# One decoder layer on one core: the embedding's projection moved from the middle to the front and kept in DRAM, the first up slab split earlier, and the gate tiles in another order

## The chip, the core and the metric

The kernel runs on one core of a Trainium2 chip. TensorE (PE) multiplies, VectorE (DVE), ScalarE (ACT) and GpSimd (POOL) work elementwise, and SyncE (SP) issues most transfers. Each has a queue of its own and takes its instructions in order. The metric is the device time of one launch in microseconds; three runs of the kernel before gave 852.27, 852.78 and 852.79, median 852.78.

## The reference

One layer over 512 tokens of 1024 features, all float32 (cut to what matters):

```python
h = _layer_norm(x, ln_in_g, ln_in_b)
proj = h @ w_in[i]
pool_in, qkv, z, beta_raw, a_raw, gate_a, gate_b = jnp.split(proj, SPLIT_POINTS, axis=-1)
y_a = _multiscale_pool(pool_in, pool_w[i], pool_scale[i])
y_b = _gated_deltanet(qkv, z, beta_raw, a_raw, ...)
mixed = jax.nn.sigmoid(gate_a) * y_a + jax.nn.sigmoid(gate_b) * y_b
h = _layer_norm(DEEPNORM_ALPHA * h + mixed @ w_out[i], ln1_g[i], ln1_b[i])
mlp = jnp.square(jax.nn.relu(h @ w_up[i])) @ w_down[i]
r = DEEPNORM_ALPHA * h + mlp
ple = jax.nn.sigmoid(r @ ple_gate_w[i]) * (p[i] @ ple_proj_w[i])
h = _layer_norm(r + ple, ln2_g[i], ln2_b[i])
```

The embedding's projection is `p[i] @ ple_proj_w[i]`: 512x256 by 256x1024. It depends on inputs alone and is used only in the last but one line, so it can be computed anywhere ahead of that. Gate is used below for `sigmoid(r @ ple_gate_w[i])`.

## The kernel before, in words

Every float32 matrix product is computed from split operands: `hi` is the operand rounded to TensorE's fast type (fp32r), `lo` the rest, and three matmuls, hi by hi, hi by lo and lo by hi, replace one. A weight slab therefore costs a transfer into a `raw` tile (512 KB), a cast on ACT to `hi` and a subtraction on DVE to `lo`, each 128 partitions by 1024. Activations that are multiplied stand with features on partitions in `act`, in hi and lo; the tokens of 128 each (four blocks, t = 0 to 3) are brought there by TensorE transposes, an ACT cast and a DVE subtraction (`to_features`, `features`).

In the order of the program:

1. The front: `warm_up` runs fourteen small matmuls on the identity, X comes in eight transfers of 256 KB, `stats` takes each block's mean and variance on DVE, POOL makes `rstd_in` and `nmr` from them, ACT normalises X, PE transposes it (`ps_in`), ACT applies gain and offset (`hf_in`), and `act` gets its hi and lo parts. During the transposes, eight more warm-up matmuls are issued. Then come the first matmuls, `ps_ba` and `ps_k`.
2. The two mixers over all heads, to about 405 us.
3. The output projection (`tok_gemm` with `wo`): weights in eight slabs, four token blocks by two column halves in PSUM; `out_done` adds the residual, does LN1's statistics and leaves the block's result in `res[t]`, followed by `to_features`. Ahead of it p is transposed (`pT`), and behind it the embedding's projection runs: 48 matmuls into `ps_pp`, eight ACT copies into `pproj` in SBUF.
4. The feed-forward network in a loop over eight column groups c of w_up (`up_tile`, `even_block`, `odd_block`) with w_down's pieces x, y, z and w (`fetch`, `onto`, `split_dn`, `product`, `gather`): sums of quarters of w_down are multiplied instead of all quarters, and `gather` puts the products together on DVE. The very first up tiles are computed in two token halves (`HALVES`) in the old form.
5. The end: `features(0)` and `features(1)` transpose the first two token blocks of the result, `product(4)` follows, then the gate's tiles: `gate_tile(t, half)` is 24 matmuls for one token block and one half of the columns. `embed` applies the sigmoid, multiplies with `pproj` and adds; `finish` is LN2.

The code states one order, but instructions are put into each engine's queue by a scheduler that simulates the program. `tc.issue_after(x)` forbids that something is issued ahead of x. PSUM and SBUF tiles come from pools with tags and a number of buffers; the next tile of a tag waits for whoever still reads the buffer that it takes.

## Time and profile before

| | |
|---|---|
| median of three runs | 852.78 us |
| profiled execution, its own time | 852.83 us |
| span of the profiled execution | 851.0 us |
| PE busy | 833.2 us (98%) |
| DVE busy | 605.9 us (71%) |
| ACT busy | 404.0 us (47%) |
| POOL busy | 90.0 us (11%) |
| mean DMA rate | 116 GB/s |

A row of the timeline gives start, length, engine, line of the kernel, operation, and tiles as output<-inputs; in brackets, how long the engine had been idle before and who ended that. Rows of repeated matmuls are folded (x5). The length of one matmul contains its fill, so successive matmuls start closer together than they are long. PEld is the weight load ahead of a matmul, PEclk the clock that TensorE was granted as a part of full speed. The lines themselves stand in the prediction.

### The profile page before, as it was taken

The page shows a single profiled execution, that of the slowest core. Times are in us where ns is not written, and L with a number is a line of the kernel's source. Part 1 is how long each engine was busy: PE and PEld are TensorE (multiplying, and loading weights), DVE is VectorE, ACT ScalarE, POOL GpSimd, SP SyncE. Part 2 cuts the span into 40 slices and gives each one's busy share as a digit, 9 for nine tenths or more (in the row PEclk, how much of TensorE's full clock was granted, in tenths as well). Part 3 has the DMA queues.
Part 4 walks back from the last instruction along what each step waited for, and adds up shares of the span by engine and source line. Part 5 has one row for each costly group of instructions (what it writes and reads, how often), then busy time and mean ns, then how long its engine had stood idle before and what let it go on. Part 6 is the DMA issues. An engine that isn't in the chain of part 4 may idle for free.

```text
span 851.0 us, 12480 instructions
## 1 busy us (share of the span) xinstructions
PE 833.2 (98%) x4848; PEld 693.9 (82%) x4848; DVE 605.9 (71%) x1185; ACT 404.0 (47%) x628; POOL 90.0 (11%) x94
## 2 busy tenths in 40 slices
PE   7999999999999999999999999999999999999996
PEld 5787888888888888888888878888888888888785
DVE  8798968759866635569369394857576767667986
ACT  5566455465563634442207555353545453634510
POOL 4061000001000000110011111111111111010000
PEclk9999999999999999999999999999999999999999
DMA  6313222321321312265316647575757566654221
GB/s 204 99 53 96 83 69 54 97 75 50 84 73 33 109 47 75 81 211 159 125 50 217 155 128 174 140 172 139 179 138 190 133 166 163 156 127 123 75 75 49
DMA packets 73196, 98.45 MB, mean 116 GB/s; under 512 B 4537, under 2 KB 48946, under 8 KB 73138
## 3 DMA queue, kind: packets, MB, share of 16 engines
q1 hardware_dynamic: 64384, 80.87, 30.0%
q0 software_dynamic: 8704, 16.78, 11.9%
q8 instruction: 38, 0.62, 0.3%
q14 instruction: 20, 0.16, 0.1%
q10 hardware_dynamic: 50, 0.01, 0.0%
HBM read 95.56 MB, written 2.10 MB: 115 GB/s over the span
## 4 chain that ended last, share of the span: by engine, by line
PE 90%; DVE 5%; ACT 2%; DMA 1%; issue 1%; POOL 0%; SPq 0%; DVEq 0%; ACTq 0%; POOLq 0%
PE ps_up L844 19%; PE ps_dnx L844 5%; PE ps_pg L844 5%; PE ps_dn L844 5%; PE ps_dny L844 5%; PE ps_dnz L844 3%; PE ps_z L67 2%; PE ps_gb L66 2%; PE ps_z L66 2%; PE ps_ga L67 2%; PE ps_gb L68 2%; PE ps_gb L67 2%; PE ps_z L68 2%; PE ps_ga L66 2%; PE ps_ga L68 2%; PE ps_q L66 1%
## 5 line engine op out<-in xcount | busy, mean ns | idle before, releaser
L844 PE MATMUL ps_up<-act,hi_up 128*128 128x512 f32 x480 | 147.8, 389 | 0.0
L844 PEld LDWEIGHTS ps_up<-act,hi_up 128*128 128x128 f32 x480 | 90.0, 188 | 18.6
L844 PE MATMUL ps_up<-act,lo_up 128*128 128x512 f32 x240 | 93.4, 389 | 0.0
L844 ACT ACTIVATE r<-ps_up 128x512 f32<-128x512 f32 x32 | 19.0, 595 | 102.4 <-PE ps_up L844 99.5
L844 POOL DMA_DIRECT2D x<-in_w_down_dram x24 | 29.0, 1210 | 273.8 <-DVE lo_dn L844 273.8
L844 PEld LDWEIGHTS ps_up<-act,lo_up 128*128 128x128 f32 x240 | 45.0, 188 | 9.4
L844 DVE TENSOR_TENSOR lo_dn<-x,hi_dn 128x1024 fp32r<-128x1024 f32 x32 | 39.0, 1220 | 8.3 <-ACT hi_dn L844 8.3
L844 PE MATMUL ps_dnx<-hi_dn,hid_s 128*128 128x512 f32 x128 | 42.3, 391 | 0.0
L844 ACT CAST hi_dn<-x 128x1024 fp32r<-128x1024 f32 x32 | 33.5, 1048 | 12.2 <-PE ps_dn L844 9.0
L844 ACT CAST hid_s<-r 128x512 fp32r<-128x512 f32 x32 | 18.3, 618 | 41.5 <-DVE r L844 41.5
L844 DVE TENSOR_TENSOR hid_a<-r,hid_a 128x256 fp32r<-128x256 f32 x16 | 6.8, 426 | 41.4 <-ACT hid_a L844 41.4
L844 PE MATMUL ps_pg<-hi_pg,act 128*128 128x512 f32 (+1 forms) x128 | 35.9, 363 | 0.0
L844 DVE TENSOR_TENSOR hid_b<-r,hid_b 128x512 fp32r<-128x512 f32 x16 | 11.1, 692 | 34.0 <-ACT hid_b L844 34.0
L844 DVE TENSOR_TENSOR lo_up<-raw_up,hi_up 128x1024 fp32r<-128x1024 f32 x28 | 33.5, 1217 | 0.0
L844 DVE TENSOR_TENSOR r<-r 128x256 f32<-128x256 f32 x64 | 27.2, 425 | 2.2
L844 ACT CAST hi_up<-raw_up 128x1024 fp32r<-128x1024 f32 x28 | 28.6, 1046 | 0.0
L844 PEld LDWEIGHTS ps_dnx<-hi_dn,hid_s 128*128 128x128 f32 x128 | 23.9, 188 | 5.7 <-DVE hid_s L844 0.4
L844 DVE TENSOR_TENSOR hid_s<-r,hid_s 128x512 fp32r<-128x512 f32 x32 | 20.7, 689 | 11.0 <-ACT hid_s L844 11.0
L844 PEld LDWEIGHTS ps_pg<-hi_pg,act 128*128 128x128 f32 x128 | 23.1, 189 | 3.8
L844 PE MATMUL ps_dnx<-lo_dn,hid_s 128*128 128x512 f32 x64 | 24.9, 389 | 0.0
L577 POOL TENSOR_TENSOR rs<-rs,mhalf 128x4 f32<-128x4 f32 x8 | 9.0, 1131 | 150.0 <-DVE rs L576 150.0
L844 DVE TENSOR_TENSOR res<-ps_dnx,res 128x512 f32<-128x512 f32 x32 | 21.0, 685 | 4.7 <-PE ps_dnx L844 4.7
(734 smaller groups left out, 2397.2 us busy)
## 6 DMA issues: line engine op xcount, KB each, us to landing
raw_up<-in_w_up_dram SPq DMA_DIRECT2D x32, 512.0 KB, 7.9
x<-in_w_down_dram POOLq DMA_DIRECT2D x24, 512.0 KB, 6.1
raw_wo<-in_w_out_dram SPq DMA_DIRECT2D x8, 512.0 KB, 3.5
x<-in_w_down_dram SPq DMA_DIRECT2D x8, 512.0 KB, 9.3
z<-in_w_down_dram SPq DMA_DIRECT2D x8, 512.0 KB
y<-in_w_down_dram SPq DMA_DIRECT2D x8, 512.0 KB, 7.7
w<-in_w_down_dram SPq DMA_DIRECT2D x8, 512.0 KB, 3.5
y<-in_w_down_dram POOLq DMA_DIRECT2D x8, 512.0 KB, 8.8
```

The lines of the kernel that those rows point to most:

```text
L66: T.matmul(ps, wh, ah, start=first, stop=False)
L67: T.matmul(ps, wh, al, start=False, stop=False)
L68: T.matmul(ps, wl, ah, start=False, stop=last)
L577: G.tensor_tensor(out=rs, in0=rs, in1=mhalf.to_broadcast([P, NT]), op=ALU.pow)
L844: return lambda *a, **k: tc.keep_in_program_order(op(*a, **k))
```

## The change

The projection of the embedding moves to the front. Directly behind the warm-up, p and its weights are loaded ahead of X, transposed and split, and `project` computes both halves; each result is copied to SBUF and written to a DRAM tile (`pproj`, eight of 256 KB). In the loop's groups 2 and 3 they are read back into SBUF tiles (`ppb`). The statistics of X, in DVE's queue, are issued behind the projection's subtractions; of those, the second slab's is on POOL. The eight warm-up matmuls among X's transposes go.

In the middle, `first_up` loads the two slabs of the first up tiles in place of the projection's weights and splits them in four pieces during the output projection. X of w_down is split (`split_dn(x, "01")`) ahead of the last two token blocks' features. Both first up tiles compute their first token half ahead of these features, and their second half behind. The tiles of the PSUM pool `pp2` are declared in another order.

At the end `gather(yb, 1, 1, SUB)` is issued ahead of the split of the gate's second slab, and the gate tile of block 1 ahead of `features(2)` and `features(3)`.

```diff
     warm_up(ps_warm, 14)
+    dp = root.enter_context(tc.tile_pool(name="dp", bufs=8, space=bass.MemoryType.DRAM))
+    ptok = mxp.tile([P, NT, 256], F32, tag="big", name="ptok")
+    dma(out=ptok, in_=p[0, 0].rearrange("(t p) c -> p t c", p=P))
+    wraw = []
+    for half in range(2):
+        raw = wp.tile([P, 2, 512], F32, tag="raw", bufs=3, name=f"raw_pp{half}")
...
+    for kb in range(2):
+        ps = tps(f"ps_pT{kb}")
+        for t in range(NT):
+            T.transpose(ps[:, t, :], ptok[:, t, kb * P:(kb + 1) * P], ident)
+        ps = ps.rearrange("p t c -> p (t c)")
+        act_last = A.copy(pT[kb][0], ps)
+        vec_last = V.tensor_tensor(out=pT[kb][1], in0=ps, in1=pT[kb][0].bitcast(F32), op=SUB)
+    wpp = []
+    for half in range(2):
...
+        with tc.issue_after(act_last.ins), tc.issue_after(vec_last.ins):
+            act_last = A.copy(hi, wraw[half])
+            sub = (G if half else V).tensor_tensor(out=lo, in0=wraw[half], in1=hi.bitcast(F32), op=SUB)
+            vec_last = vec_last if half else sub
+        wpp.append((hi, lo))
+    st_last = vec_last
...
+    def project(half):
+        hi, lo = wpp[half]
+        for t in range(NT):
+            ps = gps(f"ps_pp{half}{t}")
+            for kb in range(2):
+                ah, al = pT[kb][0][:, t * P:(t + 1) * P], pT[kb][1][:, t * P:(t + 1) * P]
+                T.matmul(ps, ah, hi[:, kb, :], start=kb == 0, stop=False)
+                T.matmul(ps, ah, lo[:, kb, :], start=False, stop=False)
+                T.matmul(ps, al, hi[:, kb, :], start=False, stop=kb == 1)
+            got = ep.tile([P, 512], F32, tag="E", bufs=8, name=f"ppc{half}{t}")
+            A.copy(got, ps)
+            pproj[t, half] = dp.tile([P, 512], F32, tag="pp", bufs=8, name=f"pproj{half}{t}")
+            dma(out=pproj[t, half], in_=got)
...
     for t in range(NT):
-        with tc.issue_after(st_last.ins) if t else nullcontext():
+        with tc.issue_after(st_last.ins):
             st_last = stats(xts[t], f"in{t}", tp1, mv_in[:, t, :])
...
-            if kb == 3:
-                with tc.issue_after(pe_last.ins):
-                    warm_up(ps_warm, (2, 2, 0, 0)[t])
...
-    pp2.tile([P, SEQ], F32, tag="g", bufs=6, name="ps_g")
...
+    pp2.tile([P, 4, P], F32, tag="tp", bufs=2, name="ps_t")
+    for i in range(2):
+        pp2.tile([P, SEQ], F32, tag="g", bufs=6, name=f"ps_g{i}")
...
+    def first_up(k0):
+
+        raw = wp.tile([P, 4, 256], F32, tag="raw", bufs=3, name=f"raw_up0_0{k0}")
+        dma(out=raw, in_=w_up[0, k0:k0 + 512, 0:256].rearrange("(a p) c -> p a c", p=P))
+        for q in range(2):
+            hi, lo = (ep.tile([P, 2, 256], F32R, tag="E", bufs=8, name=f"{n}_up0_0{k0}{q}") for n in ("hi", "lo"))
+            A.copy(hi, raw[:, 2 * q:2 * q + 2, :])
+            V.tensor_tensor(out=lo, in0=raw[:, 2 * q:2 * q + 2, :], in1=hi.bitcast(F32), op=SUB)
+            ups.append((hi, lo))
...
+        for k0 in (0, 512):
+            first_up(k0)
...
-            to_features(res[t], t, pp2, ("tp",), 2, "l1")
+            if t < 2:
+                to_features(res[t], t, pp2, ("tp",), 2, "l1")
...
+    start = [g3(f"ps_up00{i}") for i in range(2)]
+    for i in range(2):
+        up_tile(start[i], i, ups, HALVES[0])
+    w = {1: split_dn(x, "01")}
+    for t in range(2, NT):
+        features(t, "l1")
...
+        if c in (2, 3):
+            for t in range(NT):
+                got = ep.tile([P, 512], F32, tag="E", bufs=8, name=f"ppb{c - 2}{t}")
+                oS.dma_start(out=got, in_=pproj[t, c - 2])
+                pproj[t, c - 2] = got
...
-    gates = [[ups[0], split_up(raws[1], "pg01")], []]
     product(7, left, w[7], yb, True, True)
     gather(yb, 1, 1, SUB)
+    gates = [[ups[0], split_up(raws[1], "pg01")], []]
...
     first = list(gate_tile(0, 0, whole))
     gather(yb, 1, 0)
+    second = list(gate_tile(1, 0, whole))
     features(2)
     features(3)
-    second = list(gate_tile(1, 0, whole))
```

How instructions stand on the engines, at the three places. First ACT's queue at the front, before: the four blocks of X are normalised (`x`), then the first features (`hf_in`).

```order
L213 ACT_TABLE_LOAD
L213 ACTIVATE x_106<-x_106,nmr,rstd_in 128x1024
L213 ACTIVATE x_109<-x_109,nmr,rstd_in 128x1024
L213 ACTIVATE x_112<-x_112,nmr,rstd_in 128x1024
L213 ACTIVATE x_115<-x_115,nmr,rstd_in 128x512
L219 COPY pcol<-ps_prow 128x25
L233 ACTIVATE hf_in_203<-ps_in_198,pcol 128x512
L195 CAST hi_k_225<-raw_k_144 128x1024
L233 ACTIVATE hf_in_212<-ps_in_207,pcol 128x512
```

In the change, from pT's second cast on (`ppc` are copies of the projection):

```order
L162 CAST hi_pp_132<-raw_pp_110 128x1024
L162 CAST hi_pp_136<-raw_pp_112 128x1024
L179 COPY ppc_193<-ps_pp_186 128x512
L260 ACTIVATE x_140<-x_140,nmr,rstd_in 128x1024
L260 ACTIVATE x_143<-x_143,nmr,rstd_in 128x1024
L179 COPY ppc_204<-ps_pp_197 128x512
L260 ACTIVATE x_146<-x_146,nmr,rstd_in 128x1024
L179 COPY ppc_215<-ps_pp_208 128x512
L260 ACTIVATE x_149<-x_149,nmr,rstd_in 128x512
L266 COPY pcol<-ps_prow 128x25
L179 COPY ppc_226<-ps_pp_219 128x512
L239 CAST hi_k_347<-raw_k_178 128x1024
```

Five of the projection's copies (a fifth follows the last row) and the second cast of k's weights now stand ahead of the first features. On SP, at the program's start, the difference of the two queues:

```order
-L183 DMA raw_ba<-in_w_in_dram 128x8x16
-L183 DMA raw_k_142<-in_w_in_dram 128x4x256
-L183 DMA raw_k_144<-in_w_in_dram 128x4x256
...
+L143 DMA ptok<-in_p_dram 128x4x256
+L147 DMA raw_pp_110<-in_ple_proj_w_dram 128x2x512
+L147 DMA raw_pp_112<-in_ple_proj_w_dram 128x2x512
+L187 DMA x_140<-in_x_dram 128x512 x2
...
+L233 DMA dtb<-in_dt_bias_dram 128x8
+L227 DMA raw_k_176<-in_w_in_dram 128x4x256
+L227 DMA raw_k_178<-in_w_in_dram 128x4x256
+L181 DMA pproj_195<-ppc_193 128x512
```

Three transfers stand ahead of X, and k's weights behind the small loads. Third, PE at the end, before: the end of the first gate tile, the transposes of the last two blocks (`ps_rt`), and the second tile's start.

```order
L844 MATMUL ps_pg_7261<-lo_pg_7246,act 128x512
L844 MATMUL ps_pg_7261<-hi_pg_7245,act 128x512
L844 MATMUL ps_rt_7288<-ident,res_4223 128x128 x4
L844 MATMUL ps_rt_7295<-ident,res_4223 128x128 x4
L844 MATMUL ps_rt_7302<-ident,res_4224 128x128 x4
L844 MATMUL ps_rt_7309<-ident,res_4224 128x128 x4
L844 MATMUL ps_pg_7316<-hi_up_7068,act 128x512
L844 MATMUL ps_pg_7316<-lo_up_7069,act 128x512
```

In the change (`ps_pg_7331` is the second gate tile, `ps_pg_7412` the third, the first with the other half's weights):

```order
L880 MATMUL ps_pg_7331<-lo_pg_7289,act 128x512
L880 MATMUL ps_pg_7331<-hi_pg_7288,act 128x512
L880 MATMUL ps_rt_7356<-ident,res_4326 128x128 x4
L880 MATMUL ps_rt_7363<-ident,res_4326 128x128 x4
L880 MATMUL ps_rt_7370<-ident,res_4327 128x128 x4
L880 MATMUL ps_rt_7377<-ident,res_4327 128x128 x4
L880 MATMUL ps_pg_7412<-hi_pg_7384,act 128x512
L880 MATMUL ps_pg_7412<-lo_pg_7385,act 128x512
```

The transposes have moved behind the second tile, directly ahead of the third. On DVE the order there is as before:

```order
L880 TENSOR_TENSOR act<-ps_rt_7356,act 128x4x128
L880 TENSOR_TENSOR act<-ps_rt_7363,act 128x4x128
L880 TENSOR_TENSOR act<-ps_rt_7370,act 128x4x128
L880 TENSOR_TENSOR act<-ps_rt_7377,act 128x4x128
L880 TENSOR_TENSOR lo_pg_7385<-raw_pg_7296,hi_pg_7384 128x1024
L880 TENSOR_TENSOR lo_pg_7389<-raw_pg_7298,hi_pg_7388 128x1024
```

The third tile's first `lo_pg` (7385) stands behind the four subtractions from `ps_rt`.

More of the change, by code (lines that the diff above doesn't have):

```diff
@@ L7 @@
-from contextlib import ExitStack, nullcontext
+from contextlib import ExitStack
 import concourse.bass as bass
@@ L197, in k0_part @@
         return hi, lo
+    for half in range(2):
+        project(half)
     rstd_in = cst.tile([P, NT], F32, name="rstd_in")
@@ L811, in layer @@
     tok_gemm(w_out[0], lambda kb, i, t: mixed[kb][:, i, t * P:(t + 1) * P], _P2(), "g", "wo", out_done)
-    pproj = {}
-    for half in range(2):
-        hi, lo = load(ple_proj_w[0, :, 512 * half:512 * half + 512].rearrange("(a p) c -> p a c", p=P), 512,
-                      f"pp{half}")
-        for t in range(NT):
-            ps = pp2.tile([P, 512], F32, tag="g", bufs=pp2g, name=f"ps_pp{half}{t}")
-            for kb in range(2):
-                ah, al = pT[:, kb, 0, t * P:(t + 1) * P], pT[:, kb, 1, t * P:(t + 1) * P]
-                T.matmul(ps, ah, hi[:, kb, :], start=kb == 0, stop=False)
-                T.matmul(ps, ah, lo[:, kb, :], start=False, stop=False)
-                T.matmul(ps, al, hi[:, kb, :], start=False, stop=kb == 1)
-            pproj[t, half] = ep.tile([P, 512], F32, tag="E", bufs=8, name=f"pproj{half}{t}")
-            A.copy(pproj[t, half], ps)
     ph2.close()
@@ L849, in g3 @@
         return pp3.tile([P, SEQ], F32, tag="g", bufs=4, name=name)
-    perm = {i: [pp3.tile([P, SEQ], F32, tag="u", bufs=4, name=f"ps_dn{i}_{m}") for m in range(2)]
-            for i in (1, 6)}
     def wide(name):
@@ L899, in split_up, with up_tile @@
         return split(raw, name, wp, ("whi", "wlo"))
-    def up_tile(c, j, i, gr):
-        ps = g3(f"ps_up{c}{j}{i}")
-        ms = slice(i * P, (i + 1) * P)
-        first = c == 0 and j == 0
-        for c0, c1 in (HALVES if first else ((0, SEQ),)):
-            for kb in range(KB):
-                hi, lo = gr[kb // 4]
-                for q, (w, h) in enumerate(((hi, 0), (hi, 1), (lo, 0))):
-                    (T if first else oT).matmul(ps[:, c0:c1], w[:, kb % 4, ms], act[:, kb, h, c0:c1],
-                                                start=kb == 0 and q == 0, stop=kb == KB - 1 and q == 2)
+    def up_tile(ps, i, gr, cut=(0, SEQ)):
+        ms, (c0, c1) = slice(i * P, (i + 1) * P), cut
+        blocks = [(hi[:, j, ms], lo[:, j, ms]) for hi, lo in gr for j in range(hi.shape[1])]
+        for kb, (hi, lo) in enumerate(blocks):
+            for q, (w, h) in enumerate(((hi, 0), (hi, 1), (lo, 0))):
+                oT.matmul(ps[:, c0:c1], w, act[:, kb, h, c0:c1],
+                          start=kb == 0 and q == 0, stop=kb == KB - 1 and q == 2)
         return ps
@@ L962, in gather, with features @@
                 oV.tensor_tensor(out=dst, in0=dst, in1=banks[m], op=SUB)
-    def features(t):
+    def features(t, name="rt"):
         for half in range(2):
-            ps = pp3.tile([P, 4, P], F32, tag="u", bufs=4, name=f"ps_rt{t}{half}")
+            ps = pp3.tile([P, 4, P], F32, tag="u", bufs=4, name=f"ps_{name}{t}{half}")
             for a in range(4):
@@ L988, in layer @@
         left = [None, None]
-        ps = up_tile(c, 0, 0, ups[0:2])
         if fst:
-            w[1] = split_dn(x, f"{c}1")
-            onto(x, c, 0, 1)
+            ps = up_tile(start[0], 0, ups[0:4], HALVES[1])
+            ups += [split_up(raw, f"up0{n}") for n, raw in enumerate(raws)]
         else:
+            ps = up_tile(g3(f"ps_up{c}00"), 0, ups[0:2])
             gather(yb, 1, 0)
@@ L1000, in layer @@
         r2, ha = even_block(c, 0, ps)
-        ps = up_tile(c, 0, 1, ups[0:2])
+        ps = up_tile(start[1], 1, ups[0:4], HALVES[1]) if fst else up_tile(g3(f"ps_up{c}01"), 1, ups[0:2])
         w[2] = split_dn(z, f"{c}2")
@@ L1014, in layer @@
         left[0] = odd_block(c, 0, ps, r2, ha)
-        ps = up_tile(c, 1, 0, ups[2:4])
+        ps = up_tile(g3(f"ps_up{c}10"), 0, ups[-2:])
         if fst:
@@ L1018, in layer @@
         r2, ha = even_block(c, 1, ps)
-        ps = up_tile(c, 1, 1, ups[2:4])
+        ps = up_tile(g3(f"ps_up{c}11"), 1, ups[-2:])
         if fst:
```

25 lines of the change are left out of this document (13 added, 12 removed).

## The prediction

> **What bounds the kernel now.** I read the page's head first, then busy time by stretches, then the chain of waits at the start, then the timeline at the three places that the change touches.
>
> ```profile
> span 851.0 us, 12480 instructions
> ...
> PE 833.2 (98%) x4848; PEld 693.9 (82%) x4848; DVE 605.9 (71%) x1185; ACT 404.0 (47%) x628; POOL 90.0 (11%) x94
> ```
>
> TensorE is busy for 833.2 of 851.0 us. Work that leaves the middle gains its full length, and work that arrives at the front costs its full length, unless it falls into idle time. Where that lies, by stretches (length; busy time of PE, PEld, DVE, ACT, POOL; granted clock, DMA share, GB/s):
>
> ```profile
> 0.00:10.00 10.00, 6.16 (x37) 5.74 (x37) 8.51 (x20) 3.53 (x3) 6.54 (x21) 1.00 0.82 250
> 10.00:15.00 5.00, 2.97 (x21) 2.20 (x21) 3.83 (x8) 3.74 (x6) 2.42 (x5) 0.99 0.62 170
> 15.00:18.00 3.00, 3.00 (x11) 2.18 (x11) 2.28 (x5) 3.00 (x6) 0.00 (x0) 0.50 0.95 318
> ...
> 443.00:467.00 24.00, 23.68 (x149) 20.86 (x148) 22.17 (x32) 14.64 (x23) 4.42 (x3) 1.00 0.54 179
> 467.00:788.00 321.00, 321.00 (x1454) 266.31 (x1453) 212.37 (x291) 158.32 (x219) 38.95 (x32) 1.00 0.62 152
> ```
>
> PE idles 3.84 + 2.03 = 5.87 us in the first 15, and not at all in the 321 us of the feed-forward loop. So the front holds the idle time worth filling. From its chain of waits (start, length, what):
>
> ```profile
> 4.78 4.95 DMA x<-in_x_dram
> ...
> 13.62 0.79 ACT hf_in L233
> ...
> 18.76 0.44 PE ps_in L228 x4
> ```
>
> X's last piece lands at 4.78 + 4.95 = 9.73, and then a serial chain (statistics on DVE, rstd and nmr on POOL, normalising on ACT, transposes on PE) reaches the first features at 13.62.
>
> **The change, part by part. 1. The front.** Durations from the timeline (start, length, engine):
>
> ```profile
> 1.49 4.89 PE L95 MATMUL ps_warm<-ident 128*128 128x128 f32 x28 [1.49 <-POOL ident L81]
> 4.34 1.27 DVE L102 BATCH_NORM_STATS2 st_in<-x 128x6 f32<-128x512 f32 x2
> 5.95 0.24 POOL L208 TENSOR_SCALAR rstd_in<-mv_in 128x1 f32<-128x1 f32 x1 [1.68 <-DVE mv_in L103]
> ...
> 6.94 0.26 POOL L210 TENSOR_SCALAR nmr<-mv_in,rstd_in 128x1 f32<-128x1 f32 x1
> 7.24 1.24 ACT L213 ACTIVATE x<-x,nmr,rstd_in 128x1024 f32<-128x1024 f32 x1 [0.29 <-POOL nmr L210]
> ...
> 12.32 0.82 ACT L213 ACTIVATE x<-x,nmr,rstd_in 128x512 f32<-128x512 f32 x1 [0.70 <-POOL nmr L210]
> ...
> 14.29 1.03 ACT L195 CAST hi_k<-raw_k 128x1024 fp32r<-128x1024 f32 x1
> ...
> 24.41 0.39 PE L66 MATMUL ps_k<-act,hi_k 128*128 128x512 f32 x1
> 24.64 0.39 PE L67 MATMUL ps_k<-act,hi_k 128*128 128x512 f32 x1
> ...
> 26.93 0.39 PE L68 MATMUL ps_k<-act,lo_k 128*128 128x512 f32 x1
> ```
>
> A 512-wide matmul costs 24.64 - 24.41 = 0.227 us where they follow one another. The first k tile ends at 26.93 + 0.39 = 27.3; the front's cost is measured there, because PE is nearly never idle behind it.
>
> SyncE now issues ptok and two raw_pp, 3 x 512 KB, ahead of X. What the DMA engines move when they are full:
>
> ```profile
> 6.00:8.00 2.00, 0.55 (x5) 0.32 (x3) 1.95 (x4) 1.71 (x2) 1.24 (x4) 1.00 0.98 338
> ```
>
> 1.57 MB / 338 GB/s = 4.7 us, at a share of 0.98, so X cannot come beside it: its last piece lands near 14.4. Three engines then carry new work ahead of X. The warm-up ends at 6.4, the eight pT transposes near 7.4; ACT casts pT twice and hi_pp twice (about 0.55 and 1.03 each) to 10.6. DVE subtracts pT twice and splits lo_pp0 to about 10.7, and only then starts the statistics (row 4.34). POOL does lo_pp1 ahead of its first rstd. No row has a 128x1024 subtraction on POOL; the nearest, of 128x512, on POOL and on DVE (busy us, mean ns):
>
> ```profile
> L314 POOL TENSOR_TENSOR gs<-upper,glo 128x512 fp32r<-128x512 f32 x8 | 11.9, 1508 | 28.2 <-DVE glo L298 28.2
> L314 DVE TENSOR_TENSOR gs<-upper,ghi 128x512 fp32r<-128x512 f32 x8 | 6.4, 811 | 0.0
> ```
>
> POOL takes 1.508 / 0.811 = 1.86 times DVE's time. DVE does a 128x1024 in 1.21 (row 810.43 below), so 2.25 us; the ends are 1.2 (as on DVE) and 3.0 (twice 1.508). I take 2.25, by the ratio of one and the same operation.
>
> POOL is through at 10.6 + 2.25 = 12.85; rstd and nmr take 6.94 + 0.26 - 5.95 = 1.25, so X's first normalising starts near 14.1. ACT then runs in order three X blocks (1.24), the last half block (0.82), four copies of the projection (0.55, row 456.38 below), and the second hi_k (1.03), which stood behind the first features before: 3.7 + 0.8 + 2.2 + 1.0 = 7.7. First features near 21.8 instead of 13.62: **+8.2**, a little less as starts lie closer than lengths. By PE instead: when X's second block is ready, near 16.6, PE has ahead of it 30 of the 48 projection matmuls (6.8), 28 transposes (0.44 for four, 3.1) and the 40 matmuls of ba and the first k tile (9.1): 16.6 + 19.0 = 35.6 against 27.3: **+8.3**. I take **+8.0**. In other words: PE gets 48 x 0.227 = 10.9 and eight transposes, 1.0, loses eight warm-up matmuls (8 x 4.89 / 28 = 1.4), and of the 5.87 idle us only 2.5 are filled, since the projection itself must wait for lo_pp0. Ends: +4.7, if all behind X's landing keeps pace, and +10.5, if no idle time is filled.
>
> In SyncE's queue, raw_k now follows the smaller loads and waits for two of the three raw buffers, until lo_pp0 and lo_pp1 are done, near 12.9; with X landing until 14.4 it comes at 17 to 18, ahead of its casts near 19. And raw_v0a stands behind the last write of the projection, which waits for the last copy near 29: 1 us later than the front's shift alone, but its weights are first used at
>
> ```profile
> 46.11 0.40 PE L66 MATMUL ps_v<-act,hi_v0a 128*128 128x512 f32 x1
> ```
>
> so that is nothing. Eight writes of the result and eight reads of it in the feed-forward loop, 256 KB each, add 4.2 MB. The cover is the DMA share of 0.62 in 467-788, with fetches issued some ten us ahead; I cost them at nothing. Without that cover a read costs 0.26 MB / 338 GB/s = 0.8 us.
>
> **2. The middle.**
>
> ```profile
> 404.79 1.04 PE L741 MATMUL ps_pT<-ident,ptok 128*128 128x128 f32 x8
> 406.35 0.53 PE L758 MATMUL ps_wo<-hi_wo,mx 128*128 128x512 f32 x1 [0.52 <-ACT sga L711]
> ...
> 406.98 0.74 DVE L715 SCALAR_TENSOR_TENSOR sga<-ps_lift,pcol,sga 128x512 f32<-128x512 f32 x1
> ...
> 452.13 1.31 PE L822 MATMUL ps_pp<-hi_pp,pT 128*128 128x512 f32 x5
> 452.14 1.07 ACT L118 CAST act<-ps_l 128x512 fp32r<-128x512 f32 x2
> ...
> 455.68 1.28 DVE L119 TENSOR_TENSOR act<-ps_l,act 128x512 fp32r<-128x512 f32 x2
> ...
> 456.38 1.09 ACT L826 COPY pproj<-ps_pp 128x512 f32<-128x512 f32 x2
> ...
> 465.44 0.48 PE L911 MATMUL ps_up<-act,hi_up 128*128 128x256 f32 x2
> ...
> 477.04 0.63 PE L844 MATMUL ps_up<-act,hi_up 128*128 128x512 f32 x2
> ```
>
> The pT transposes (1.04) go, but gain nothing: with the PSUM tiles declared in another order, the first ps_wo lies in the bank that ps_lift held, and waits for DVE's sga, 406.98 + 0.74 = 407.7, instead of 406.35: **+1.4**. All of PE's work is queued behind it. If ACT's sga still ended the wait, it would be 0; those are the ends.
>
> From the last output-projection matmul to the first 512-wide up matmul now pass 477.04 - 452.13 = 24.9 us. In the change: 96 half-width matmuls, 477.04 - 465.44 = 11.6; the 16 transposes of the last two token blocks, 1.7 (804.09 - 802.42 below has sixteen); about 0.75 of waiting for the second block's subtraction, which 10.9 us of projection covered; and about 1.5 behind the last transposes, where a cast (half of 1.07), a subtraction (half of 1.28) and their hand-overs stand bare. Sum 15.5, **-9.4**. The last block's statistics must come earlier for that. They do, as six 128x1024 subtractions leave DVE, which was busy for 22.17 of 24 us; the first half's 5.8 us of up matmuls cover the rest. Ends: no waits, -11.6; and the late X of rival D. Middle together: **-8.0**.
>
> **3. The end.**
>
> ```profile
> 794.15 0.47 PE L844 MATMUL ps_dny<-hi_dn,hid_b 128*128 128x512 f32 x1 [1.30 <-DVE res L844]
> ...
> 802.42 1.91 PE L844 MATMUL ps_rt<-ident,res 128*128 128x128 f32 x16
> 804.09 0.47 PE L844 MATMUL ps_pg<-hi_up,act 128*128 128x512 f32 x1
> ...
> 806.09 2.36 DVE L844 TENSOR_TENSOR lo_pg<-raw_pg,hi_pg 128x1024 fp32r<-128x1024 f32 x2
> ...
> 810.43 1.21 DVE L844 TENSOR_TENSOR lo_pg<-raw_pg,hi_pg 128x1024 fp32r<-128x1024 f32 x1
> ```
>
> The gather goes ahead of one such lo_pg on DVE, so product 4 starts 1.1 earlier, near 793.0. But the second gate tile goes ahead of the transposes of the last two token blocks. A gate tile is 24 x 0.227 = 5.44: the two now end near 801.3 and 806.7, and the transposes start at 806.7 instead of 802.42, 4.3 later. ACT's and DVE's orders are unchanged: the casts and subtractions from ps_rt stand ahead of the splits of the second half's gate weights, which so come 4.3 later too: the first lo_pg is done at 806.09 + 1.2 + 4.3 = 811.6, the third at 810.43 + 1.2 + 4.3 = 815.9; the fourth slab's transfer starts when the first is split, 3.5 us before its own split, which ends near 817.5. The third gate tile ran from 804.09 + 5.44 = 809.5 to 815.0. It could now start at 808.4, waits 3.1 us, stops again for the third and fourth slab, and has five matmuls (1.1) behind 817.5: it ends near 818.6. **+3.6**. What follows keeps that distance. Ends: -1.1 and +4.7, the second if the gather gains nothing.
>
> **Sum:** 8.0 - 8.0 + 3.6 = +3.6 on the profiled execution's 852.83 (span 851.0), which is 0.05 above the median 852.78: **856.4**.
>
> **The rivals.** A: the front costs X's delay alone, +4.7. For it speaks that ACT is busy for only 3.53 + 3.74 of the first 15 us, against it that the projection's copies and the second hi_k are queued in ACT ahead of the features. 4.7 - 8.0 + 3.6: 853.1, no change. B, on the other side: the third gate tile does not stall, and the end keeps its -1.1. Its place is DVE's queue behind the transposes; it decides by whether the first lo_pg is done when PE comes, at 808.4. For it speaks only that ACT and DVE have idle time there; the unchanged queues speak against it. 8.0 - 8.0 - 1.1: 851.7, not slower. A and B together: 848.4. C, the clock: gaps near 3 us arise at ps_wo (407.7 - 404.8) and at the third gate tile. The granted clock was 0.50 in 15-18, behind the front's gaps, which cost 1.5 us of full speed. Twice that: 859.4. [...] D: X of w_down comes late. ACT now splits it ahead of the last features (transfers, KB each, median us to landing):
>
> ```profile
> x<-in_w_down_dram SPq DMA_DIRECT2D x8, 512.0 KB, 9.3
> ...
> w<-in_w_down_dram SPq DMA_DIRECT2D x8, 512.0 KB, 3.5
> ```
>
> At 3.5 us it is there in time, at 9.3 the casts of the last two blocks start 3.9 late: 860.3.
>
> **How the numbers follow.** This kernel's measurement cannot tell a change of about 0.2%, 1.7 us, from none. Chances: forecast 0.47, A 0.12, B 0.13, A with B 0.10, C 0.10, D 0.08. Slower: forecast, C and D, less 0.03 of the forecast's own spread, 0.62. Same: A and some two thirds of B, 0.20. Faster: the rest, 0.18. The range, 849.5 to 860.5, leaves out most of A with B and half of C and D; the forecast's own is 853.5 to 859.
>
> **What would show it.** Right: the first hf_in near 21.5 and the first k tile's end near 35; ps_wo behind DVE's sga; the first 512-wide up matmul at the old time within 1 us; ps_pg with about 3 us of idle time released by lo_pg, near 808. Wrong: X's last piece landing before 12; no wait ahead of the third gate tile; a granted clock below 0.9 in the middle; ACT waiting for X of w_down near 455.

## The result, and the profile after

Four runs of the changed kernel gave 858.39, 860.18, 860.59 and 861.65, median **860.38 us**; the kernel before took 852.78 beside it. The ratio is 1.008, interval 1.0066 to 1.0095: slower by 7.6 us, where 3.6 were forecast. The profiled execution took 860.59, near the median. The page's head:

```profile
span 858.8 us, 12504 instructions
...
PE 833.7 (97%) x4840; PEld 693.3 (81%) x4840; DVE 604.9 (70%) x1186; ACT 403.6 (47%) x630; POOL 92.5 (11%) x95
```

TensorE's busy time is what it was (833.2), though a half-speed stretch at the front (clock 0.50 in 15 to 18 us) has gone and another has come in the middle (0.50 in 419 to 421); nearly all of the 7.8 us of span is new idle time (25.1 against 17.8). The table of waits, TensorE's rows, says where (total, times, longest):

```profile
PE ps_wo L805 <- DVE sga L759: 2.8, 1, 2.8
PE ps_pg L880 <- DVE lo_pg L880: 2.0, 2, 1.3
PE ps_pg L880 <- ACT hi_pg L880: 1.8, 1, 1.8
PE ps_in L275 <- ACT x L260: 1.6, 2, 1.0
PE ps_pp L175 <- ACT hi_pp L162: 1.5, 1, 1.5
...
PE ps_gb L66 <- DVE zs L730: 1.4, 1, 1.4
```

The timeline of TensorE at the places of the forecast (start, length, line, operation, tiles, and in brackets the idle time before and who ended it):

```profile
36.56 0.43 PE L298 MATMUL ps_bat<-ident,bat 32*128 32x32 f32 x4 [0.20 <-ACT bat L295]
...
398.82 0.50 PE L66 MATMUL ps_gb<-act,hi_gb3a 128*128 128x512 f32 x1 [1.43 <-DVE zs L730]
...
418.26 0.69 PE L805 MATMUL ps_wo<-hi_wo,mx 128*128 128x512 f32 x1 [2.83 <-DVE sga L759]
...
421.73 0.44 PE L807 MATMUL ps_wo<-hi_wo,mx 128*128 128x512 f32 x1
...
465.45 0.28 PE L823 MATMUL ps_wo<-hi_wo,mx 128*128 128x256 f32 x1
...
481.09 0.63 PE L880 MATMUL ps_up<-act,hi_up 128*128 128x512 f32 x2
...
796.67 0.47 PE L880 MATMUL ps_dny<-hi_dn,hid_b 128*128 128x512 f32 x1 [0.18 <-DVE res L880]
...
814.08 0.50 PE L880 MATMUL ps_pg<-hi_pg,act 128*128 128x512 f32 x1 [1.77 <-ACT hi_pg L880]
815.34 0.50 PE L880 MATMUL ps_pg<-lo_pg,act 128*128 128x512 f32 x1 [0.76 <-DVE lo_pg L880]
819.66 0.50 PE L880 MATMUL ps_pg<-lo_pg,act 128*128 128x512 f32 x1 [1.28 <-DVE lo_pg L880]
```

The same instructions of the kernel before, and how much later each is now:

| TensorE's instruction | before | after | later by |
|---|---|---|---|
| `ps_bat`, right behind the first k tile | 27.52 | 36.56 | 9.0 |
| first `ps_gb` of slab 3a | 388.34 | 398.82 | 10.5 |
| first `ps_wo` | 406.35 | 418.26 | 11.9 |
| the ninth `ps_wo` | 408.35 | 421.73 | 13.4 |
| last `ps_wo` | 452.01 | 465.45 | 13.4 |
| first up matmul of 512 columns | 477.04 | 481.09 | 4.05 |
| product 4 | 794.15 | 796.67 | 2.5 |
| the third gate tile's last wait | 812.59 | 819.66 | 7.1 |
| end of the span | 851.0 | 858.8 | 7.8 |

So the front cost 9.0, the middle gave back 13.4 - 4.05 = 9.4, and the end cost 7.8 - 4.05 = 3.7: these three the forecast had. Two things it didn't have stand between: 1.5 us at `ps_gb`, and 1.5 us over the first nine `ps_wo`. (From the first wide up matmul to product 4 pass 317.1 us before and 315.6 in the change, where 1.1 less were forecast for the gather. In the two profiles of the kernel before with the gather moved, see below, it is 316.4, so that about half of the 1.5 us is the gather's and half the loop's. The last 0.7 us, behind the third gate tile, were not followed up.)

### The profile page after: what moved, and what is told of

Its sections match the earlier page's. It is cut to its first block, busy times and chain, and to the rows that moved or that the text cites. A ratio compares the mean times of both kernels' runs of the same rounds, so it can differ in the third digit from the quotient of the medians.

```text
span 858.8 us, 12504 instructions
## 1 busy us (share of the span) xinstructions
PE 833.7 (97%) x4840; PEld 693.3 (81%) x4840; DVE 604.9 (70%) x1186; ACT 403.6 (47%) x630; POOL 92.5 (11%) x95
## 4 chain that ended last, share of the span: by engine, by line
PE 88%; DVE 6%; ACT 2%; issue 2%; DMA 1%; POOL 1%; SPq 0%; DVEq 0%; POOLq 0%; ACTq 0%
PE ps_up L880 20%; PE ps_dnx L880 5%; PE ps_dn L880 5%; PE ps_dny L880 5%; PE ps_pg L880 5%; PE ps_dnz L880 3%; PE ps_ga L67 2%; PE ps_ga L66 2%; PE ps_ga L68 2%; PE ps_gb L66 2%; PE ps_gb L68 1%; PE ps_gb L67 1%; PE ps_q L66 1%; PE ps_q L68 1%; PE ps_z L66 1%
## 5 line engine op out<-in xcount | busy, mean ns | idle before, releaser
L880 PE MATMUL ps_up<-act,hi_up 128*128 128x512 f32 (+1 forms) x544 | 159.7, 377 | 1.5 <-DVE act L119 0.6
L880 PEld LDWEIGHTS ps_up<-act,hi_up 128*128 128x128 f32 x544 | 100.0, 188 | 20.7 <-DVE act L119 0.8
L880 PE MATMUL ps_up<-act,lo_up 128*128 128x512 f32 (+1 forms) x272 | 102.4, 376 | 0.0
L880 PEld LDWEIGHTS ps_up<-act,lo_up 128*128 128x128 f32 x272 | 51.2, 188 | 9.4
L880 DVE TENSOR_TENSOR lo_up<-raw_up,hi_up 128x1024 fp32r<-128x1024 f32 x30 | 35.9, 1217 | 0.0
L880 ACT CAST hi_up<-raw_up 128x1024 fp32r<-128x1024 f32 x30 | 30.6, 1049 | 0.0
L880 PE MATMUL ps_pg<-lo_pg,act 128*128 128x512 f32 (+1 forms) x64 | 23.6, 368 | 2.0 <-DVE lo_pg L880 2.0
```

Of the source, the lines that this page charges most:

```text
L880: return lambda *a, **k: tc.keep_in_program_order(op(*a, **k))
```

## The experiments

Each time is a median beside the kernel before on the same chip. As the latter varied from 852.6 to 853.2 between chips, differences to it are compared. A profile is one execution, and the executions of one kernel lie up to 3.8 us apart, so a profile's rows need not add up to a median.

**The end: the second gate tile behind the last transposes again**, the rest of the change as it was:

```diff
-    second = list(gate_tile(1, 0, whole))
     features(2)
     features(3)
+    second = list(gate_tile(1, 0, whole))
```

> The change with one part undone: the transposes of the last two token blocks go ahead of the second gate tile again, as before; the gather stays ahead of the split. Theory (the end's loss is the place of the transposes: casts and subtractions from ps_rt block the splits of the second half's weights in ACT's and DVE's queues): the idle times before the third gate tile (1.77 + 0.76 + 1.28 us) go, a wait of about 1 us for DVE's last gather appears at the transposes instead, and the time falls by 3.5 to 4 us from the change's 860.4, to about 856.5. Rival (the third tile waits for the transfer of its weights): no gain, 860.4 within 1 us.

Measured 856.07 (before 853.15; ratio 1.003, 1.0018 to 1.0041): 2.9 above before, 4.7 less than the change. TensorE's only wait in that place:

```profile
802.88 1.97 PE L880 MATMUL ps_rt<-ident,res 128*128 128x128 f32 x16 [0.88 <-DVE res L880]
```

The three waits of the third gate tile are gone, so the order of these lines of code cost what the forecast had put on it (3.6 and the gather's 1.1), and most of the earlier gather's gain is lost into 0.88 us of waiting for `res`. The median fell by more than the 3.5 to 4 us expected. The profiled execution, 853.69, is the shortest of ten and has neither `y`'s wait nor the half clock behind `ps_wo`.

**The end: the gate's splits ahead of the last transposes.** If it is the order in ACT's and DVE's queues, the gate tile may stay early, as long as the splits don't stand behind the transposes' casts:

```diff
     second = list(gate_tile(1, 0, whole))
+    for n in range(3):
+        gates[1].append(split(raws[n], f"pg1{n}", tp3, ("dhi", "dlo")))
     features(2)
     features(3)
-    for n in range(4):
-        gates[1].append(split(raws[n], f"pg1{n}", tp3, ("dhi", "dlo")))
-        if n == 1:
-            embed(0, 0, *first[0])
+    gates[1].append(split(raws[3], "pg13", tp3, ("dhi", "dlo")))
+    embed(0, 0, *first[0])
```

> The change, with the splits of the second half's gate weights moved in the program: the first three ahead of the last two blocks' features, the fourth directly behind them. Order of the tensor engine unchanged. Theory (queue order on ACT and DVE): the third gate tile starts without a wait, and the time falls by 4.9 us from 860.4, to 855.5. Rival (the weights' transfer): ACT or DVE waits for raw_pg instead and 2 us or more of the idle time stay, 857.5 or more.

Measured 855.01 (before 853.15; 1.0021, 1.0011 to 1.0032), 1.9 above before and 5.7 less than the change. The transposes stand late and nothing waits, behind them either:

```profile
809.59 1.91 PE L880 MATMUL ps_rt<-ident,res 128*128 128x128 f32 x16
```

That is the mechanism: the stall came from what is queued behind the transposes' casts on two other engines, not from the tile's place on TensorE.

**The gather alone**, moved in the kernel before:

```diff
-    gates = [[ups[0], split_up(raws[1], "pg01")], []]
     product(7, left, w[7], yb, True, True)
     gather(yb, 1, 1, SUB)
+    gates = [[ups[0], split_up(raws[1], "pg01")], []]
```

> The kernel before with one part of the change alone: the gather ahead of the split of the gate's second slab. Theory: product 4 starts 1.1 us earlier, but the transposes behind the first gate tile then wait for DVE's last gather, which has not moved, so that nearly all is lost: 852.6, no change. Rival (the gather is worth its 1.1 us by itself): 851.7.

Measured 852.45 (before 853.15; 0.9992, 0.9982 to 1.0002): no change that can be told.

```profile
793.12 0.47 PE L844 MATMUL ps_dny<-hi_dn,hid_b 128*128 128x512 f32 x1 [0.17 <-DVE res L844]
...
802.43 1.97 PE L844 MATMUL ps_rt<-ident,res 128*128 128x128 f32 x16 [0.90 <-DVE res L844]
```

Product 4 starts 1.0 earlier, and 0.9 of it turns into a wait for `res` ahead of the next transposes (802.42 before, 802.43 now).

**The middle: the PSUM tiles declared as before:**

```diff
-    pp2.tile([P, 4, P], F32, tag="tp", bufs=2, name="ps_t")
-    for i in range(2):
-        pp2.tile([P, SEQ], F32, tag="g", bufs=6, name=f"ps_g{i}")
+    pp2.tile([P, SEQ], F32, tag="g", bufs=6, name="ps_g")
```

> The change with the PSUM tiles of the output projection declared as before. Theory (the first output-projection matmul waits for DVE's sga because of the bank that it was given; behind 2.83 us of idle time the clock is halved for some 3.4 us): the wait falls to about 1.5 us, ended by ACT's sga, the granted clock stays at 1.00, and the time falls by 1.4 + 1.6 = 3.0 us, to about 857.4. Rival 1 (the clock falls after any such gap): only 1.4 us, 859. Rival 2 (the wait is for the mixers' last result whatever the bank): no gain.

Measured 858.17 (before 853.15; 1.0057, 1.0042 to 1.0072), 5.0 above before, 2.6 less than the change: between the theory's 3.0 and rival 1's 1.4. ACT's `sga` ends the wait again, with 1.42 us less of it, and the clock behind it stays at 1.00, so rival 2 falls; in this profile the clock fell at another place (last section). The first `ps_wo`:

```profile
417.27 0.50 PE L803 MATMUL ps_wo<-hi_wo,mx 128*128 128x512 f32 x1 [1.41 <-ACT sga L755]
```

**The front: three transfers ahead of X, nothing else**, in the kernel before; their data go unused:

```diff
     warm_up(ps_warm, 14)
+    ahead = mxp.tile([P, NT, 256], F32, tag="big", name="ahead0")
+    dma(out=ahead, in_=p[0, 0].rearrange("(t p) c -> p t c", p=P))
+    for half in range(2):
+        ahead = mxp.tile([P, 2, 512], F32, tag="big", name=f"ahead{half + 1}")
+        dma(out=ahead, in_=ple_proj_w[0, :, 512 * half:512 * half + 512].rearrange("(a p) c -> p a c", p=P))
     xts = []
```

> The kernel before with three transfers of 512 KB (p and the projection's weights, into tiles that nothing reads; the projection stays in the middle and loads its own) ahead of X, and nothing else. It measures what the change's front pays for X's later arrival alone. Theory 1 (X's delay is half of the front's price, the rest is the work in the queues): X's last piece lands 4 to 5 us later, the first features move by about 4.5, and the time rises to 857.3. Theory 2 (the front's price is the projection's work alone and X's delay is hidden): 853 to 854. Theory 3 (X's delay is all of it): the rise is 8 to 9, to 861.5.

Measured 857.18 (before 852.81; 1.0049, 1.0032 to 1.0067), 4.4 later. The chain of waits and busy time by stretches:

```profile
8.41 4.95 DMA x<-in_x_dram
```

```profile
6.00:9.00 3.00, 1.02 (x9) 0.79 (x7) 0.77 (x2) 0.00 (x0) 0.00 (x0) 1.00 1.05 389
9.00:12.00 3.00, 0.00 (x0) 0.00 (x0) 2.93 (x7) 2.04 (x2) 1.64 (x5) 0.51 1.04 372
```

X's last piece lands at 13.36 instead of 9.73, 3.6 later and not 4.7: the DMA moved 372 to 389 GB/s where 338 was assumed. Theory 1 has the time (857.3). But the profiled execution, 855.55, is the shortest of the four, and its `ps_bat` stands at 30.33, only 2.8 later than in the kernel before. So the transfers alone cost between 2.8 us, by this profile, and 4.4, by the medians: a third to a half of what the whole new front costs.

**The front: the work.** In the change, 20 of the 24 matmuls of the projection's second half are left out:

```diff
             for kb in range(2):
                 ah, al = pT[kb][0][:, t * P:(t + 1) * P], pT[kb][1][:, t * P:(t + 1) * P]
+                if half and kb:
+                    continue
-                T.matmul(ps, ah, hi[:, kb, :], start=kb == 0, stop=False)
+                T.matmul(ps, ah, hi[:, kb, :], start=kb == 0, stop=half == 1)
+                if half:
+                    continue
```

> The change with 20 of the 24 matmuls of the projection's second half left out (one of six for each token tile stays, so that half's result is not the reference's); every transfer, cast, subtraction, copy and eviction stays. Theory 1 (TensorE's own work sets the front once X is there): the 20 matmuls at about 0.23 us each go from the front, the end of the first k tile comes 4.6 us earlier than in the change (about 31.8 instead of 36.4), and the kernel takes 855.8. Theory 2 (X's arrival and LayerNorm's chain on ScalarE set the front, and the projection's matmuls fill what would be idle): the first features stay where they are, TensorE's rows show 2 to 4 us of idle time behind ScalarE's x in 15 to 25 us, the k tile comes at most 2 us earlier, and the kernel takes 858.5 to 860.4.

Measured 858.20 (before 852.60; 1.0062, 1.0048 to 1.0076), 5.6 above before, 2.0 less than the change. Theory 1 falls: TensorE has 4.6 us less to do and the first k tile's end comes only 1.3 us earlier (`ps_bat` at 35.22 instead of 36.56). This profile's projection began 0.5 later, at 9.77 instead of 9.27; as `ps_bat` comes 27.3 us behind the projection's first matmul in all six profiles with the change's front, 1.8 us are the matmuls' own:

```profile
21.99 0.50 PE L177 MATMUL ps_pp<-hi_pp,pT 128*128 128x512 f32 x1 [0.94 <-ACT ppc L183]
22.67 1.99 PE L279 MATMUL ps_in<-ident,x 128*128 128x128 f32 x12 [0.18 <-ACT hf_in L281]
...
35.22 0.37 PE L302 MATMUL ps_bat<-ident,bat 32*128 32x32 f32 x3 [0.20 <-ACT bat L299]
```

By stretches (length; busy time of PE, PEld, DVE, ACT, POOL; clock, DMA share, GB/s):

```profile
15.00:20.00 5.00, 3.45 (x19) 2.55 (x19) 3.35 (x8) 4.94 (x8) 3.96 (x9) 1.00 0.62 202
20.00:25.00 5.00, 3.83 (x20) 2.25 (x20) 3.00 (x5) 5.00 (x10) 0.00 (x0) 1.00 0.92 265
```

ACT is busy for 9.94 of these 10 us: X's normalising, the copies `ppc`, the casts and `hf_in` follow one another in its queue, and the first `hf_in` stands at 21.81, as far behind the projection's start as in the change (21.34). Theory 2 comes near: the first features stay, TensorE idles for 2.7 us in 15 to 25, and the time is 0.3 below its range. What the rows add is that ACT's queue, with the copies in it, sets the front next, and not X's arrival.

**The same, and these four copies on DVE:**

```diff
-            A.copy(got, ps)
+            (V.tensor_copy if half else A.copy)(got, ps)
```

> As the run before (20 of the 24 matmuls of the projection's second half left out, so that half's result is not the reference's), and the four evictions of that half are copied by VectorE and not by ScalarE. Theory (with those matmuls gone ScalarE is what sets the front: it was busy for 5.00 of 5.00 us in 20 to 25, and TensorE waited 0.94 for its copy ppc and 0.18 for hf_in): the first hf_in starts 0.6 to 1.2 us earlier than 21.81, TensorE's wait for ppc goes, the end of the first k tile comes 1 to 2.3 us earlier than 35.0, and the kernel takes 856.0 to 857.2. Rival (X's arrival sets it, through the statistics and the normalising): first hf_in and k tile stay within 0.3 us, 858.2.

Measured 856.25 (before 852.69; 1.0047, 1.0031 to 1.0064), 3.6 above before. `ps_bat` is at 34.49, 0.7 earlier (0.85 from the projection's start, 9.89 here), less than the theory's 1 to 2.3, and the first `hf_in` 0.3 earlier, at 21.48. ACT has gaps now, and DVE none:

```profile
20.00:25.00 5.00, 4.18 (x23) 2.64 (x23) 5.00 (x9) 4.38 (x9) 0.00 (x0) 1.00 0.91 269
```

The rest of the 2.0 us between these two kernels is not the copies': in their profiles it is the clock behind the wait at `ps_wo` (last section), 47.2 us from the first `ps_wo` to the last against 45.6. So the median's 856.25, which lies in the theory's range, does not bear the theory out. With one engine relieved the next one holds, first ACT, then, by its full row, DVE: 4.6 us of matmuls gained 1.8 at `ps_bat`, 2.4 us of copies 0.85.

**All in the middle.** The change with nothing at the front, the projection behind the output projection again, its results to DRAM from there; PSUM tiles as before and the gate's splits mended:

```diff
+    for half in range(2):
+        hi, lo = load(ple_proj_w[0, :, 512 * half:512 * half + 512].rearrange("(a p) c -> p a c", p=P), 512,
+                      f"pp{half}")
...
+            got = tp2.tile([P, DM], F32, tag="y", bufs=4, name=f"ppc{half}{t}")[:, 0:512]
+            A.copy(got, ps)
+            pproj[t, half] = dp.tile([P, 512], F32, tag="pp", bufs=8, name=f"pproj{half}{t}")
+            dma(out=pproj[t, half], in_=got)
```

> The change without its front: the projection stays behind the output projection, where it was, with its results written to DRAM as in the change; the early first up slab, the split of X of w_down, the order of the last features, the gather and the gate tiles are the change's, with the bank order of before and the splits ahead of the casts at the end. Theory (the tensor engine is full in the middle, so that moving the projection is worth no more than what is idle at the front): all waits of the middle are covered by the projection, and the time is that of the kernel before less 1.1 us of the end and some 0.5 of the middle, 851.3. Rival (the middle gains by itself, from the early slab): 849 or less.

Measured 856.74 (before 852.81; 1.004, 1.0027 to 1.0053): 5.4 above the theory. Of its timeline, ACT, then TensorE, then SyncE's queue:

```profile
469.22 1.05 ACT L863 CAST hi_dn<-x 128x1024 fp32r<-128x1024 f32 x1 [5.86 <-DMA x<-in_w_down_dram]
470.18 2.04 ACT L863 CAST act<-ps_l 128x512 fp32r<-128x512 f32 x4
```

```profile
471.78 0.39 PE L863 MATMUL ps_up<-act,hi_up 128*128 128x256 f32 x1 [1.58 <-ACT act L863]
473.38 0.58 PE L863 MATMUL ps_up<-act,hi_up 128*128 128x256 f32 x1 [1.22 <-DVE act L863]
```

```profile
454.74 8.97 SPq L844 DMA_DIRECT2D pproj<-ppc  x8
463.80 0.39 SPq L863 DMA_DIRECT2D raw_up<-in_w_up_dram  x1
464.28 0.52 SPq L863 DMA_DIRECT2D x<-in_w_down_dram  x1
```

This is the prediction's rival D, in another kernel. The eight writes hold SyncE's queue until 463.71, X of w_down is issued behind them at 464.28, ACT waits for it for 5.86 us with the last features' casts queued behind, and TensorE stops twice; from 473 to 475 us its clock is then 0.54. In the change itself X's wait was 0.66. So this run doesn't price the projection's place: my way of building it brought a stall of its own.

**Half and half**: the first half's projection at the front, the second in the middle.

```diff
-    for half in range(2):
-        project(half)
+    project(0)
...
+    for half in (1,):
+        hi, lo = load(ple_proj_w[0, :, 512 * half:512 * half + 512].rearrange("(a p) c -> p a c", p=P), 512,
+                      f"pp{half}")
```

> As the change without its front, but one half of the projection (24 of 48 matmuls, two of three transfers) at the front and the other half in the middle. Theory (the front fills little idle time): X comes 3.1 us later, the front costs about 5 us and the middle gains 5.4: 851, as without it. Rival (half of the work fits into the front's idle time): the front costs only X's 3.1 us, 849.

Measured 856.58 (before 852.81; 1.0033, 1.002 to 1.0047). Neither time came. The front is 6.2 later (`ps_bat` at 33.71) for half of the work, nearer to the theory's 5 than to the rival's 3.1, and the middle shows the same stall behind four writes:

```profile
470.55 1.05 ACT L902 CAST hi_dn<-x 128x1024 fp32r<-128x1024 f32 x1 [5.73 <-DMA x<-in_w_down_dram]
```

**The change, mended**: the projection at the front, the PSUM tiles declared as before, the gate's splits ahead of the last transposes (the two edits shown above).

> The change with both mended parts: the bank order of before, and the splits of the second half's gate weights ahead of the last casts. Theory (the two losses are independent: 5.4 and 2.2 us measured apart): 860.4 - 7.6 = 852.8, no change against the kernel before. Rival (they share the same idle time): 854.5 or more.

Measured 851.74 (before 852.81; 0.9987, 0.9977 to 0.9996), 8.7 less than the change relative to before. The two edits alone gave 2.6 and 5.7, so their gains add up, as the theory had it, and the time lies 1.1 below its 852.8. To learn whether this last gain is the front's or the end's, it ran again, beside the kernel before with the mended end alone (the edits of the gather and of the gate's splits; the projection in the middle):

> The mended change once more (the change with the PSUM declaration as before and the first three splits of the second gate slab ahead of the last transposes), beside the kernel before with the mended end alone. Theory (the move is worth nothing): 851.7, within 0.5 of the mended end alone. Rival (the move gains): 1 us or more below the mended end alone. A second rival (the 1.1 us below the kernel before was chance): equal to the kernel before, 852.8.

> The kernel before, projection in the middle as it was, with two things of the changed kernel's end only: the last gather ahead of the first gate tile's split, and the first three splits of the second gate slab ahead of the last transposes, the fourth and the first embedding behind them. Theory (the projection's move is worth nothing, and the 1.1 us that the mended change gained over the kernel before is the end's alone): 1.1 below the kernel before, about 851.7 to 851.9, the same as the mended change, with the last product's first matmul 1.1 us earlier and no wait at the third gate tile. Rival (the move itself gains about 1 and the end nothing, since the gather alone gave no difference that could be measured): 852.8, the kernel before, and the mended change about 1 below this kernel.

The mended change: 851.96 (before 852.60; 0.9992, 0.9983 to 1.0001). The mended end alone: 851.88 (0.9996, 0.9987 to 1.0005). The two are equal, 0.1 us apart with intervals of about 0.8 to either side. Against the kernel before the mended change gained 1.1 us the first time, with an interval that leaves out no change, and 0.6 the second time, with one that doesn't; the mended end gained 0.7, likewise within its interval. What remains of the change, the projection's place together with the early up slab and the new order of the last features, is worth nothing that can be measured. The profiles of these two kernels, with mean clocks of 0.998 (the mended end alone) and 0.997, and with 1.00 in the mended change behind the wait at `ps_wo` (412 to 420 us), show why:

| TensorE's instruction | mended end alone | mended change | later by |
|---|---|---|---|
| `ps_bat` | 27.02 | 36.46 | 9.4 |
| last `ps_wo` | 451.66 | 460.97 | 9.3 |
| first up matmul of 512 columns | 476.30 | 476.49 | 0.2 |
| product 4 | 792.69 | 792.04 | -0.65 |
| end of the span | 849.5 | 849.3 | -0.2 |

What is lost at the front comes back in the middle. (A wait of 1.41 at the first `ps_wo` is still in the mended change; the kernel before has 0.52 there.)

## Why the prediction was right or wrong

The direction held, slower, and with it the mechanism at all three places. The size did not: 860.38 lies above the forecast's own 853.5 to 859, and only 0.12 below the end of the range, 860.5; two of the four runs, 860.59 and 861.65, lie beyond it. That the range held is luck, since 3.0 of the missing 4.0 us are two losses that some profiles have and others lack. In the profiled execution the 3.6 became 7.8, by these terms (as rounded they add up to 7.7):

| step | forecast | measured |
|---|---|---|
| front, at the first k tile | +8.0 | +9.0 |
| wait of the first `ps_wo` | +1.4 | +1.4 |
| clock behind it | none (rival C) | +1.5 |
| last `ps_wo` to the first wide up matmul | -9.4 | -9.4 |
| end: gather, then gate tile | +3.6 | +3.7 |
| y's late transfer | not seen | +1.5 |

**The front.** The chain was right to the tenth in places: X's first normalising at 14.12 (forecast 14.1), the first `hf_in` at 21.34 (near 21.5). The subtraction on POOL took 2.48 (2.25); it ends at 12.73 and `rstd_in` starts at 12.83, though DVE had the first block's statistics at 11.92, and what that order on POOL costs was not tried. The two ways of working the front out, by ACT's queue 8.2 and by PE's work 8.3, were near each other, and the run without 20 matmuls shows that both bounds are real: with PE's lowered by 4.6, ACT's holds at 1.8 less. By PE's way the first k tile was to end 19.0 us behind X's second block, at 35.6; that block was transposed at 16.73 (16.6), with 30 projection matmuls still to come, as forecast, and the tile ended at 36.37, 19.6 later. In the prediction's other words the mis-sized term is the idle time filled, 2.5. Busy time by stretches of the change:

```profile
0.00:10.00 10.00, 7.01 (x39) 6.30 (x39) 5.41 (x12) 4.08 (x5) 3.61 (x13) 1.00 0.82 284
10.00:15.00 5.00, 3.94 (x17) 2.93 (x16) 4.90 (x11) 1.63 (x3) 4.30 (x6) 1.00 1.05 294
15.00:20.00 5.00, 3.93 (x22) 3.20 (x23) 3.34 (x7) 4.93 (x9) 3.48 (x9) 1.00 0.70 243
20.00:25.00 5.00, 5.00 (x32) 4.26 (x31) 2.85 (x6) 5.00 (x10) 0.00 (x0) 1.00 0.95 279
```

TensorE idles for 2.99 + 1.06 + 1.07 = 5.1 us, against 5.87 before: 0.75 was filled. The net of added work, 10.9 + 1.0 - 1.4 = 10.5, less these 0.75, would be 9.75. That it was 9.0 fits the half clock of the kernel before in 15 to 18 us, which made TensorE's work there longer, while the change's rows show 1.00. But that half clock is not what kept the kernel before from an earlier `ps_bat`. The run of the gather alone has the same front at full clock, and its `ps_bat` is at the same place:

```profile
15.00:18.00 3.00, 2.89 (x16) 2.03 (x17) 2.32 (x5) 3.00 (x6) 0.00 (x0) 1.00 0.93 283
```

```profile
27.43 0.43 PE L254 MATMUL ps_bat<-ident,bat 32*128 32x32 f32 x4 [0.21 <-ACT bat L251]
```

Over all profiles, `ps_bat` stands at 26.92 to 27.52 with the front of before (four profiles) and at 36.08 to 37.43 with the change's (six, whose spread all lies ahead of the projection's first matmul), so that the front's price is 8.6 to 10.5 by the pair of profiles that one takes. The projection filled little of the gaps: it has its own transfers, casts and subtractions to wait for, and X's chain then waits behind these.

**The middle.** The wait at `ps_wo` came as forecast, 2.83 behind DVE's `sga`, and the declaration alone takes it away. What was wrong is the step that gave this gap no price beyond its length, which was the author's estimate and holds in some of the runs only (last section), and left what the clock might add to a rival with a chance of 0.10. Busy time by stretches, the clock in the last column but two:

```profile
418.00:419.00 1.00, 0.74 (x2) 0.65 (x3) 0.90 (x2) 0.03 (x1) 0.00 (x0) 0.71 0.63 148
419.00:421.00 2.00, 2.00 (x6) 1.54 (x6) 0.69 (x1) 0.58 (x1) 0.00 (x0) 0.50 0.77 257
421.00:422.00 1.00, 1.00 (x4) 0.79 (x3) 0.00 (x0) 0.00 (x0) 0.00 (x0) 0.59 0.03 12
422.00:424.00 2.00, 2.00 (x10) 1.66 (x9) 0.00 (x0) 0.00 (x0) 0.00 (x0) 1.00 0.00 0
```

The clock is halved behind the gap, and from the first `ps_wo` to the ninth 1.5 us are lost, the price that rival C put on one such gap. Half of C happened in this profile, at `ps_wo` and not at the gate tile. The stage behind was forecast at 15.5 and took 481.09 - 465.45 - 0.12 = 15.5 (0.12 for the last matmul itself). Its waits (0.58, 0.34 and 0.57) sum to 1.5 where 0.75 and 1.5 were put in, and the matmuls and transposes took 14.0 where 11.6 + 1.7 were; that the two errors cancel to the tenth is luck. X of w_down was waited for 0.66, not 3.9: D fell here, and its mechanism decided two of the experiments.

**The end.** Gate tile, queue order, three waits: as worked out. 1.77 + 0.76 + 1.28 = 3.8 us of waiting against 3.1 and two further stops forecast; both A (the front at 4.7) and B (no stall) fell with these rows. The run with the splits ahead shows that B's price is right: from product 4 to the end its profile takes 57.2 us and the change's 62.1, 4.9 less, where B was 4.7 below the forecast. The medians' 5.7 hold more than this stall.

**What no step had** is y. DVE's row (start, length, idle before):

```profile
391.30 0.81 DVE L713 TENSOR_SCALAR y<-y,mv_in,rstd_in 128x1024 f32<-128x1024 f32 x1 [4.00 <-DMA y<-in_x_dram]
```

and the same four transfers in both kernels, before (first) and after (KB each, median us to landing), each row of its own trace:

```profile
y<-in_x_dram SPq DMA_DIRECT2D x4, 512.0 KB, 8.9
```

```profile
y<-in_x_dram SPq DMA_DIRECT2D x4, 512.0 KB, 10.1
```

They were issued 8.9 us later than before, as everything there, and landed 1.2 later still. DVE waited 4.0 (2.41 before), its queue was late, and TensorE stopped for 1.43. The profile of the kernel with the gate's splits ahead shows 1.17 of it, the one with the PSUM order of before 1.20, and the mended change, which is both of these edits together, none in either of its two profiles. In all fourteen profiles the two go together: in these three the transfers land after 9.7 to 10.1 us and DVE waits 3.7 to 4.0, in the eleven others they land after 8.4 to 9.1, DVE waits 2.3 to 2.7, and TensorE doesn't stop. As nothing of that stage differs between the mended change and its two halves, it looks like a thing that varies from run to run; why was not settled.

## What to carry to other kernels

Idle time at the front is worth something only to work whose inputs are there before the gap. The projection brought its own transfers, casts and subtractions, which queue ahead of the first chain and move it: 10.5 us of work cost 9.0 there, and 9.4 were gained where it had been. When something moves on one engine, look at what stands behind its consumers in the other engines' and SyncE's queues: the order of a few lines cost 3.8 us of waits, a PSUM declaration 1.4, and eight writes ahead of one fetch 2.8. When two bounds come out equal in a forecast, lowering one gains only what the other leaves: here 1.8 of 4.6 us.
